# Three weight chunks' splits set behind the convolution's first-half taps and behind the first normalisation (two-layer decoder trunk, one core)

## The chip, the cores and the metric

The kernel runs on one core of a Trainium2 chip. The metric is device time of one execution in microseconds (us). The kernel before ran three times: 524.99 us median, 523.45 to 526.51.

## What is computed

Two residual layers over a stream of 512 tokens by 1024 channels. Layer 0 is attention; the change doesn't touch it. Layer 1, where the change lies, is cut here to what matters:

```python
def conformer_conv_layer(x, norm_g, w_in, conv_w, conv_b, ln_g, ln_b, w_out):
    h = rms_norm(x, norm_g)
    val, glu_gate, z = jnp.split(h @ w_in, 3, axis=-1)
    u = val * jax.nn.sigmoid(glu_gate)
    u = lax.conv_general_dilated(
        u, conv_w, window_strides=(1,), padding=((CONV_WIDTH - 1, 0),),
        dimension_numbers=('NWC', 'WIO', 'NWC'), feature_group_count=CONV_CH) + conv_b
    u = jax.nn.silu(layer_norm(u, ln_g, ln_b)) * jax.nn.silu(z)
    return x + u @ w_out
```

The convolution is depthwise and causal with 31 taps; the layer norm runs over all 1024 channels of a token, so no token can be normalised before the convolution of all eight channel tiles (128 channels each) is done for it.

## The kernel before

**Weights.** All weights are cut into 36 chunks of 1024 rows by 256 columns (1 MB). A chunk is loaded in fp32 into one of two buffers `wst` (`load_w`, line 152, issued by SyncE), and then split into a high and a low part (`split_w`, lines 155 to 180), since TensorE multiplies in a shorter float format and the kernel adds three products per matmul to get fp32 accuracy (`ch_mm`, `tok_mm`). Chunks 28 to 31 hold layer 1's columns for z; 33, 34, 32, 35 hold the output projection's four column groups 0, 1, 2, 3 (`OUTW`). For chunks 33, 34 and 35 the split is three steps: Pool issues a DMA that copies `wst` into the high part and rounds it (line 169: `whi` for 33 and 34, `wx` for 35); ScalarE writes minus the chunk into the low part (line 175: `wlo`, `wx`); Pool issues a second DMA that subtracts by adding `wst` onto it (line 179). Both DMAs go through Pool's one queue (q0 of the page). A `wst` buffer is free for the next load only when the ScalarE step and both DMAs are done. The function `ahead(n)` (lines 806 to 811) splits the chunks up to n-1 that are not split yet, and starts one more load after each: `ahead(34)` splits 33 and loads 34, `ahead(35)` splits 34 and loads 35, `ahead(36)` splits 35. With two buffers, 34 loads into the buffer of 32, and 35 into that of 33.

**Convolution.** Each channel tile's 31 taps are shared out: VectorE does some as multiply-adds into `s` (line 765), the rest are a ScalarE scaling into one of six buffers `tm` (line 774) and a Pool addition onto `pacc` (line 775; the first of these taps is written by ScalarE straight into `pacc`, line 771). VectorE adds both sums (line 782), TensorE transposes to token order (`conv_out`, line 795), VectorE takes statistics (line 797), ScalarE copies to `ctok` (line 798). The last two channel tiles, 6 and 7, are done in two halves of 256 tokens, so that the normalisation and projection of the first 256 tokens can start before the second half's convolution is done. The taps of their first half are written at lines 954 to 964, the z projections of chunks 28 to 30, with `ahead(34 + c)` after each, at 965 to 967.

**Order.** Up to line 1011 a scheduler orders each engine's queue. From line 1012 on the order of TensorE, VectorE, ScalarE and Pool is the order of the code: conv_out of tile 6 (first half), z of tile 6, conv_out of 7, the token statistics `norm_stats(0)` with the power of -0.5 on Pool (line 904, `lnr`), z of tile 7 in two pieces, `norm_cols` on VectorE (line 910), transposes back `ng_t` (line 921, `tp`), and then four rounds p = 0 to 3: ScalarE's SiLU (`ng_s`, line 927, `c`), VectorE's product with z (line 932), ScalarE's high part (`ng_u`, line 935, `u`), VectorE's low part (line 938), and TensorE's 24 output matmuls of the round for column groups 0 and 1 (line 360, into banks `st`, `o`, `mm`, `mm`). `na()` and `nd()` put the second half's taps between these, on ScalarE with Pool and on VectorE. Rounds 1 and 2 begin on TensorE with the transposes of the round after. Then come column groups 2 and 3, and the second half in the same way.

Of the kernel before, what the change touches and what calls it, by code (L numbers as in the profile page):

```python
# [13 lines left out]
AF = mybir.ActivationFunctionType  # L14
ALU = mybir.AluOpType
# [79 lines left out]
def tile_kernel(ctx: ExitStack, tc: tile.TileContext, x, xt, w, small0, small1, l1_norm, out):  # L95
# [7 lines left out]
    V, A, G, T, SY = nc.vector, nc.scalar, nc.gpsimd, nc.tensor, nc.sync  # L103
# [10 lines left out]
    def bank(tag, bufs):  # L114
        return ps.tile([P, 512], F32, tag=tag, name=tag, bufs=bufs)
# [4 lines left out]
    def stbank():  # L120

        return bank("st", 1)
# [8 lines left out]
    def sbank():  # L131
        return bank("s", 2)
# [94 lines left out]
    def fetch(i):  # L227
        if i < len(wsrc):
            raw[i] = load_w(*wsrc[i], 4 if i == 0 else 1)

    def split(i):
        if i < len(wsrc):
            wts[i] = split_w(raw.pop(i), rings[i], SPLIT_ENG(i, nc), APARTS if i in DMAS else 4 if i == 0 or 17 <= i < 24 else WPARTS, i in CAST)
# [34 lines left out]
    for i in range(2):  # L268
# [3 lines left out]
        for h in range(2):  # L272
            o, s = slice(8 * h, 8 * h + 8), slice(8 - 8 * h, 16 - 8 * h)
# [49 lines left out]
    for t in range(NT):  # L323
        hn = v0[:, (t % 2) * KC * P:(t % 2 + 1) * KC * P].rearrange("p (k t) -> p k t", k=KC)
        ts = slice(t * P, (t + 1) * P)
        for h in range(2):
            ks = slice(h * 4, h * 4 + 4)
            V.tensor_tensor(hn[:, ks], xts[t][:, ks], gcol[:, ks, None].to_broadcast([P, 4, P]),
                            op=ALU.mult)
            hp[2 * t + h] = hpart = A.activation(hhi[:, ks, ts], hn[:, ks], AF.Copy)  # L330
            V.tensor_tensor(hlo[:, ks, ts], hn[:, ks], hhi[:, ks, ts].bitcast(F32),
                            op=ALU.subtract)
        if t == 0:
            split(0)
    for t in range(NT):
        with tc.issue_after(hp[JO[t]].ins):
            A.activation(xs[t], xs[t], AF.Square, accum_out=ssx[:, t:t + 1])
        v = small.tile([P, 1], F32, tag="vv", name="vv")
# [127 lines left out]
    last = [None] * 4  # L466
# [280 lines left out]
    def conv_steps(ct, acc, pacc, n0, n):  # L747

        u = ups[ct % NU]
        nv = CONV - (POOLT[ct] if ct < KC - NLATE else POOLH[ct, n0 // HT])  # L750
        o = slice(n0, n0 + n)

        def tap(i):
            return u[:, OFF + i + n0:OFF + i + n0 + n], cw[:, ct, i:i + 1]

        first = []

        def vstep(i):
            v, w = tap(i)
            if i == 0:  # L760
                first.append(l1.tile([P, S], F32, tag="first", name="first", bufs=FB))
                V.tensor_scalar(first[0][:, :n], v, w, cbias[:, ct:ct + 1], op0=ALU.mult,
                                op1=ALU.add)
            else:
                V.scalar_tensor_tensor(acc[:, o], v, w, first[0][:, :n] if i == 1 else acc[:, o],  # L765
                                       op0=ALU.mult, op1=ALU.add)

        def astep(i):
            v, w = tap(i)
            if i == nv:  # L770
                A.activation(pacc[:, o], v, AF.Copy, scale=w)
                return
            tm = l1.tile([P, S], F32, tag="tm", name="tm", bufs=TMB)
            A.activation(tm[:, :n], v, AF.Copy, scale=w)  # L774
            G.tensor_tensor(pacc[:, o], pacc[:, o], tm[:, :n], op=ALU.add)  # L775

        return ([partial(vstep, i) for i in range(nv)],
                [partial(astep, i) for i in range(nv, CONV)])

    def conv_final(acc, pacc, n0, n):  # L780
        o = slice(n0, n0 + n)
        return lambda: V.tensor_tensor(pacc[:, o], acc[:, o], pacc[:, o], op=ALU.add)

    def conv(ct, acc, pacc, n0, n):
        v, a = conv_steps(ct, acc, pacc, n0, n)
        v[0]()
        a[0]()
        for f in v[1:] + a[1:]:
            f()
        last[3] = conv_final(acc, pacc, n0, n)()  # L790

    def conv_out(ct, pacc, t0=0, n=NT):
        pt = tpbank()
        for t in range(t0, t0 + n):
            last[1] = T.transpose(pt[:, t * P:(t + 1) * P], pacc[:, t * P:(t + 1) * P], identf)
        for t in range(t0, t0 + n):
            V.bn_stats(stats[:, t, ct, :], pt[:, t * P:(t + 1) * P])
        A.activation(ctok[:, t0:t0 + n, ct * P:(ct + 1) * P],
                     pt[:, t0 * P:(t0 + n) * P].rearrange("p (t c) -> p t c", t=n), AF.Copy)

    def new_pacc():
        return l1.tile([P, S], F32, tag="pacc", name="pacc", bufs=2)
# [3 lines left out]
    def ahead(n):  # L806
        while nsp[0] < n:
            split(nsp[0])
            nsp[0] += 1
            fetch(nf[0])  # L810
            nf[0] += 1
# [26 lines left out]
    def z_chunk(i, c):  # L838
        for j in range(2):
            z_unit(i, 2 * c + j)  # L840
# [39 lines left out]
    for c in range(1, 4):  # L880
# [4 lines left out]
        for j in range(2):  # L885
# [3 lines left out]
            acc, pacc = sbank(), new_pacc()  # L889
# [16 lines left out]
    def norm_cols(h, c):  # L906

        cs = slice(c * D // 2, (c + 1) * D // 2)
        for t in (2 * h, 2 * h + 1):
            V.tensor_scalar(ctok[:, t, cs], ctok[:, t, cs], mv[:, t, 0:1], rs[:, t:t + 1],  # L910
                            op0=ALU.subtract, op1=ALU.mult)
# [50 lines left out]
            f()  # L962
    for ct in late:
        conv_final(*ends[ct], 0, HT)()
    for c in range(3):
        z_chunk(28 + c, c)
        ahead(34 + c)

    (v6, a6), (v7, a7) = (conv_steps(ct, *ends[ct], HT, HT) for ct in late)
    vsteps = v6[:V6]  # L970
# [2 lines left out]
    n = max(len(v6), len(v7))  # L973
# [19 lines left out]
    def na():  # L993
        ca(next(aq))

    def nd():
        cv(next(dq))

    def z_mm(i, ct, po=None, ks=range(KC)):
        if po is None:  # L1000
            po = mmbank()
        ch_mm(po, nhi, nlo, wts[i], ct % 2, ks=ks)
        return po

    def z_act(ct, po):
        A.activation(zs[:, ct, :], po, AF.Silu)
# [5 lines left out]
    with tc.manual_schedule(engines=engs):  # L1012
        conv_out(6, ends[6][1], 0, 2)
        z6 = z_mm(31, 6, None, range(Z6))
        na()
        nd()
        conv_out(7, ends[7][1], 0, 2)
        z_mm(31, 6, z6, range(Z6, KC))
        na()
        z_act(6, z6)  # L1020
        norm_stats(0)
        z7 = z_mm(31, 7, None, range(ZK))
        na()
        nd()
        norm_cols(0, 0)
        ng_t(0, 0)
        ng_t(0, 1)
        z_mm(31, 7, z7, range(ZK, KC))
        norm_cols(0, 1)
        banks = [stbank(), bank("o", 1), bank("mm", 2), bank("mm", 2)]  # L1030
        units = [(c, t) for c in range(2) for t in range(2)]
        for p in range(4):
            k = 2 * p
            ng_s(0, k)
            ng_s(0, k + 1)
            na()
            nd()
            ng_m(0, k)
            ng_m(0, k + 1)
            ng_u(0, k)  # L1040
            ng_u(0, k + 1)
            if p == 0:
                z_act(7, z7)
            na()
            nd()
            ng_l(0, k)
            ng_l(0, k + 1)
            if p == C34:
                hi = main.tile([P, KC, WC], F32R, tag="big", name="hi", bufs=3)
                G.dma_start(hi.rearrange("p k n -> p (k n)"), w_ap(*wsrc[32], 0, KC))  # L1050
                wts[32] = hi, wts[32][1]
            if p in (1, 2):
                ng_t(0, p + 1)
            for (c, t), po in zip(units, banks):
                out1_mm(c, t, po, (2 * p, 2 * p + 1))
        for (c, t), po in zip(units, banks):
            out1_add(c, t, po)
        ca(99)
        cv(99)
        def unit(c, t, f=None):  # L1060
            po = mmbank()
            out1_mm(c, t, po)
            return lambda: out1_add(c, t, po)
        turn[0] = 0
        u = None
        for it in SEQ:
            w = None
            if it[0] == "c":
                conv_out(int(it[1]), ends[int(it[1])][1], 2, 2)
                if it == "c7":  # L1070
                    norm_stats(1)
            elif it == "n":
                norm_cols(1, 0)
                ng_t(1, 0)
                ng_t(1, 1)
                norm_cols(1, 1)
            else:
                w = unit(int(it[0]), int(it[1]))
            if u:
                u()  # L1080
            u = w
        for k in range(4):
            ng_s(1, k)
            ng_m(1, k)
            ng_u(1, k)
            ng_l(1, k)
            if k == 1 and u:
                u()
        units = [(c, 2 + t) for c in range(2) for t in range(2)]
        banks = [bank("mm", 2), bank("mm", 2), stbank(), bank("o", 1)]  # L1090
        for p in range(4):
            if p in (1, 2):
                ng_t(1, p + 1)
                for k in (2 * p + 2, 2 * p + 3):
                    ng_s(1, k)
                    ng_m(1, k)
                    ng_u(1, k)
                    ng_l(1, k)
            for (c, t), po in zip(units, banks):
                out1_mm(c, t, po, (2 * p, 2 * p + 1))  # L1100
        for (c, t), po in zip(units, banks):
            out1_add(c, t, po)
        turn[0] = 0
        for c in (2, 3):
            for t in (2, 3):
                unit(c, t)()
# [80 lines left out]
```

## Time and profile before

| | |
|---|---|
| median of three runs | 524.99 us (523.45 to 526.51) |
| the profiled execution | 525.7 us, of which the span of the trace is 523.9 us |
| granted TensorE clock, mean | 0.984 |
| busy: TensorE / weight loads / VectorE / ScalarE / Pool | 505.9 / 462.0 / 375.8 / 329.8 / 232.3 us |
| first half's taps, normalisation and rounds | about 424 to 482 us of the span |
| second half's | to 523.9 us |

The page divides the span into 40 slices of 13.1 us with the busy share of each engine in tenths. The waits view says who waited for whom, in us in total, number of times, and the longest. The chain of waits follows the last instruction back to what released it. The timeline lists instructions with start, length and, in brackets, the idle time before them with its releaser. The windows view gives busy time per engine, the granted clock (1.00 is full) and the share of the DMA engines for a stretch.

### The profile page before, as it was taken

What the parts mean: (1) busy time and instruction counts of PE and PEld (TensorE: products, weight loads), DVE (VectorE), ACT (ScalarE), POOL (GpSimd) and SP (SyncE); (2) the same over time, 40 slices, a digit from 0 to 9 for tenths busy, and PEclk for the clock granted to TensorE, in tenths of its full rate; (3) what the DMA queues carried; (4) which work ended last, traced back from release to release, by engine and by line L of the source; (5) the groups of instructions that cost most, each with busy time, mean ns of one, the idle gap of its engine ahead of it and who ended that gap; (6) DMA issues with size and microseconds to landing.
All of it is one profiled execution on the core that took longest, in us unless ns stands there. A gap on an engine that the chain in (4) does not pass through costs nothing.

```text
span 523.9 us, 9734 instructions
## 1 busy us (share of the span) xinstructions
PE 505.9 (97%) x3683; PEld 462.0 (88%) x3683; DVE 375.8 (72%) x788; ACT 329.8 (63%) x668; POOL 232.3 (44%) x255
## 2 busy tenths in 40 slices
PE   6999999999999999999999999999999999779997
PEld 3999998987889988788779999999999887559997
DVE  6856577856565587586696256999999997778741
ACT  3846687876555785576374735998686755478230
POOL 4166545010323143223202113879998875777200
PEclk8999999999999999999999999999999999879999
DMA  7742222202122233303219578488999799962111
GB/s 264 306 180 83 81 81 102 76 30 82 61 102 81 81 125 99 138 10 114 102 41 398 124 213 233 89 210 290 230 305 255 203 261 314 265 171 101 41 49 43
DMA packets 16566, 79.05 MB, mean 151 GB/s; under 512 B 1988, under 2 KB 4352, under 8 KB 8712
## 3 DMA queue, kind: packets, MB, share of 16 engines
q1 hardware_dynamic: 12776, 51.17, 26.8%
q0 software_dynamic: 3744, 27.26, 21.7%
q8 instruction: 29, 0.48, 0.4%
q14 instruction: 17, 0.14, 0.1%
HBM read 50.07 MB, written 2.14 MB: 100 GB/s over the span
## 4 chain that ended last, share of the span: by engine, by line
PE 72%; DMA 12%; DVE 5%; ACT 5%; POOL 3%; issue 2%; SPq 0%; POOLq 0%; ACTq 0%
PE mm L360 30%; DMA wst<-in_w_dram 7%; PE mm L369 6%; PE mm L370 6%; PE mm L371 6%; PE st L360 4%; PE o L602 3%; PE tp L525 3%; POOL pacc L775 2%; PE o L360 2%; PE s L509 2%; DMA lo<-wst 2%; PE s L511 2%; DMA wlo<-wst 2%; DMA wx<-wst 2%
## 5 line engine op out<-in xcount | busy, mean ns | idle before, releaser
L775 POOL TENSOR_TENSOR pacc<-pacc,tm 128x256 f32<-128x256 f32 (+1 forms) x125 | 120.2, 982 | 16.3 <-ACT tm L774 10.5
L765 DVE SCALAR_TENSOR_TENSOR s<-u,parts,s 128x256 f32<-128x256 f32 (+1 forms) x211 | 108.2, 571 | 0.5
L360 PE MATMUL mm<-whi,hhi 128*128 128x256 f32 (+1 forms) x352 | 100.2, 292 | 3.1 <-ACT hhi L330 2.9
L360 PE MATMUL mm<-whi,hlo 128*128 128x256 f32 (+1 forms) x352 | 99.4, 289 | 0.0
L360 PE MATMUL mm<-wlo,hhi 128*128 128x256 f32 (+1 forms) x352 | 99.0, 289 | 0.0
L774 ACT ACTIVATE tm<-u,parts 128x256 f32<-128x256 f32 (+1 forms) x125 | 66.2, 571 | 14.7 <-POOL pacc L775 14.2
L360 PEld LDWEIGHTS mm<-whi,hhi 128*128 128x128 f32 x352 | 66.9, 193 | 4.7 <-ACT hhi L330 3.4
L360 PEld LDWEIGHTS mm<-whi,hlo 128*128 128x128 f32 x352 | 66.7, 193 | 0.2
L360 PEld LDWEIGHTS mm<-wlo,hhi 128*128 128x128 f32 x352 | 66.6, 193 | 0.2
L173 ACT ACTIVATE whi<-wst 128x512 fp32r<-128x512 f32 (+2 forms) x77 | 49.3, 707 | 8.8 <-DMA wst<-in_w_dram 7.8
L522 ACT ACTIVATE p<-p,nm 128x128 f32<-128x128 f32 (+3 forms) x64 | 35.8, 559 | 26.9 <-DVE nm L521 26.3
L517 POOL TENSOR_TENSOR cb<-cb,mask 128x128 f32<-128x128 f32 x32 | 15.4, 485 | 77.4 <-DVE nm L521 48.8
L177 POOL TENSOR_TENSOR wlo<-wst,whi 128x512 fp32r<-128x512 f32 (+1 forms) x22 | 31.0, 1417 | 38.3 <-ACT whi L173 38.3
L177 DVE TENSOR_TENSOR wlo<-wst,whi 128x512 fp32r<-128x512 f32 (+1 forms) x50 | 40.4, 840 | 9.9 <-ACT whi L173 9.8
L369 PE MATMUL mm<-nhi,wx 128*128 128x256 f32 (+1 forms) x104 | 33.8, 325 | 0.0
L371 PE MATMUL mm<-nhi,wx 128*128 128x256 f32 (+1 forms) x104 | 32.9, 316 | 0.0
L370 PE MATMUL mm<-nlo,wx 128*128 128x256 f32 (+1 forms) x104 | 32.8, 316 | 0.0
L370 PE MATMUL mm<-nlo,whi 128*128 128x256 f32 (+1 forms) x104 | 31.9, 307 | 0.0
L369 PE MATMUL mm<-nhi,whi 128*128 128x256 f32 (+1 forms) x104 | 31.8, 307 | 0.0
L371 PE MATMUL mm<-nhi,wlo 128*128 128x256 f32 (+1 forms) x104 | 31.7, 306 | 0.0
L395 POOL TENSOR_TENSOR rq<-vq,mhalf 128x16 f32<-128x16 f32 x8 | 26.2, 3281 | 5.0 <-DVE vq L393 4.9
L525 PE MATMUL tp<-identf,p 128*128 128x128 f32 x160 | 28.1, 275 | 0.4 <-ACT pt L533 0.3
(292 smaller groups left out, 1434.8 us busy)
## 6 DMA issues: line engine op xcount, KB each, us to landing
wst<-in_w_dram SPq DMA_DIRECT2D x33, 1024.0 KB, 5.2
wx<-wst POOLq DMA_DIRECT2D x13, 1024.0 KB, 7.9
wlo<-wst POOLq DMA_DIRECT2D x8, 1024.0 KB, 8.9
whi<-wst POOLq DMA_DIRECT2D x3, 1024.0 KB, 5.9
wst<-in_w_dram SPq DMA_DIRECT2D x2, 1040.0 KB, 4.7
xs<-in_x_dram SPq DMA_DIRECT2D x4, 512.0 KB, 9.4
cb<-cdram SPq DMA_DIRECT2D x8, 256.0 KB, 3.7
x<-in_x_dram SPq DMA_DIRECT2D x4, 512.0 KB, 7.2
```

Of the source, the lines that this page charges most:

```text
L173: A.activation(hi[:, ks], st[:, ks], AF.Copy)
L177: (V if eng is G and parts == 4 and k % 4 and V0 else eng).tensor_tensor(lo[:, ks], st[:, ks], hi[:, ks].bitcast(F32), op=ALU.subtract)
L360: T.matmul(po, a[:, k, ts], b[:, k, :n], start=first and i == 0, stop=last and i == len(prods) - 1)
L369: T.matmul(po, whi[:, k, cs], a, start=k == 0, stop=False)
L370: T.matmul(po, whi[:, k, cs], b, start=False, stop=False)
L371: T.matmul(po, wlo[:, k, cs], a, start=False, stop=k == KC - 1)
L395: G.tensor_tensor(r, v, mhalf[:, :16].rearrange("p (t h) -> p t h", t=NT), op=ALU.pow)
L522: A.activation(p[:, :w], p[:, :w], AF.Exp, bias=nm, scale=-1.0, accum_out=sm[:, h, t:t + 1])
L525: T.transpose(tp[:, j * P:(j + 1) * P], p[:, j * P:(j + 1) * P], identf)
L765: V.scalar_tensor_tensor(acc[:, o], v, w, first[0][:, :n] if i == 1 else acc[:, o], op0=ALU.mult, op1=ALU.add)
L774: A.activation(tm[:, :n], v, AF.Copy, scale=w)
L775: G.tensor_tensor(pacc[:, o], pacc[:, o], tm[:, :n], op=ALU.add)
```

## The change

The splits of chunks 33 and 34 get a condition that they be issued only after the last first-half tap on ScalarE and on Pool (`taps`, the last ones of tile 7). The split of chunk 35 is taken out of the loop and put behind `norm_cols(0, 1)`, in the part whose order is the code's. `last[3]`, which held VectorE's final addition and was read nowhere, now holds the Pool tap.

```diff
-            A.activation(tm[:, :n], v, AF.Copy, scale=w)
-            G.tensor_tensor(pacc[:, o], pacc[:, o], tm[:, :n], op=ALU.add)
+            last[2] = A.activation(tm[:, :n], v, AF.Copy, scale=w)
+            last[3] = G.tensor_tensor(pacc[:, o], pacc[:, o], tm[:, :n], op=ALU.add)
...
-        last[3] = conv_final(acc, pacc, n0, n)()
+        conv_final(acc, pacc, n0, n)()
...
+    taps = last[2].ins, last[3].ins
     for c in range(3):
         z_chunk(28 + c, c)
-        ahead(34 + c)
+        if c < 2:
+            with tc.issue_after(taps[0]), tc.issue_after(taps[1]):
+                ahead(34 + c)
...
         z_mm(31, 7, z7, range(ZK, KC))
         norm_cols(0, 1)
+        ahead(36)
         banks = [stbank(), bank("o", 1), bank("mm", 2), bank("mm", 2)]
```

No instruction is added or taken away, and TensorE's, VectorE's and SyncE's queues keep their order. On Pool, in the stretch from the first half's taps to round 0, `pacc` rows are taps, `whi`, `wlo` and `wx` rows the DMAs of chunks 33, 34 and 35, `lnr` the power of the first half's norm:

```order
-L775 TENSOR_TENSOR pacc<-pacc,tm 128x256
+L775 TENSOR_TENSOR pacc<-pacc,tm 128x256 x15
 L169 DMA whi<-wst 128x2048
-L775 TENSOR_TENSOR pacc<-pacc,tm 128x256
 L179 DMA wlo<-wst 128x2048
 L169 DMA whi<-wst 128x2048
+L179 DMA wlo<-wst 128x2048
+L775 TENSOR_TENSOR pacc<-pacc,tm 128x256 x3
+L904 TENSOR_TENSOR lnr<-lnv,mhalf 128x2
+L775 TENSOR_TENSOR pacc<-pacc,tm 128x256 x7
+L169 DMA wx<-wst 128x2048
+L179 DMA wx<-wst 128x2048
```

The four DMAs of chunks 33 and 34, which stood among the taps, now stand together behind all of the first half's; the two of chunk 35, which stood ahead of `lnr`, stand behind it and behind seven of the second half's taps.

On ScalarE, at the end of that stretch, `wx` is the low part of chunk 35, `ctok` the copy of tile 7's first half, `zs` the SiLU of z of tile 6 and `c` the SiLU that opens round 0 (line 1006 has become 1010):

```order
-L175 ACTIVATE wx<-wst 128x2048
 L798 ACTIVATE ctok<-tp 128x2x128
-L1006 ACTIVATE zs<-mm 128x512
+L1010 ACTIVATE zs<-mm 128x512
 L774 ACTIVATE tm<-u_3240,parts 128x256 x7
+L175 ACTIVATE wx<-wst 128x2048
 L927 ACTIVATE c<-tp,parts 128x256 x2
```

Chunk 35's step stood ahead of the copy, and now stands directly ahead of round 0's SiLU. The two `wlo` steps of chunks 33 and 34 have likewise moved from among ScalarE's first-half taps to behind the last of them.

## Prediction

> **What bounds the kernel now.** First the page: TensorE is busy nearly all the time, so the holes in its row are the place to look.
>
> ```profile
> span 523.9 us, 9734 instructions
> PE 505.9 (97%) x3683; PEld 462.0 (88%) x3683; DVE 375.8 (72%) x788; ACT 329.8 (63%) x668; POOL 232.3 (44%) x255
> PE   6999999999999999999999999999999999779997
> ```
>
> The two 7s are 445 to 471 us, just where the change works. Next the waits, 420 to 500 us:
>
> ```profile
> DVE pacc L782 <- POOL pacc L775: 6.5, 3, 5.4
> ACT wx L175 <- DMA wst<-in_w_dram: 6.2, 1, 6.2
> DVE ctok L910 <- POOL lnr L904: 3.7, 2, 3.2
> PE tp L921 <- DVE ctok L910: 3.6, 2, 3.3
> PE tp L795 <- DVE pacc L782: 3.5, 1, 3.5
> ```
>
> TensorE has two holes. For 3.5 us it waits on VectorE's final sum, which waits on Pool's taps, which stand behind the DMAs of chunk 33 and 34 that wait for their loads. For 3.3 us it waits on the first norm, whose `lnr` stands on Pool behind chunk 35's DMA, which waits for ScalarE's step and that for its load. The chain that ended last says the same, and shows that one resource runs through it all: loads and copies of the weights.
>
> ```profile
> 424.56 10.89 DMA lo<-wst
> 435.52 6.04 DMA wst<-in_w_dram
> ...
> 449.05 9.78 DMA wst<-in_w_dram
> ...
> 469.04 1.50 PE st L360 x6
> ...
> 473.19 1.02 ACT c L927 x2
> ```
>
> After each hole TensorE's granted clock is halved (in these rows of the windows view it stands ahead of the DMA share and the GB/s):
>
> ```profile
> 449.10:452.50 3.40, 3.40 (x9) 2.62 (x9) 3.33 (x10) 2.76 (x8) 3.09 (x5) 0.51 1.15 255
> 462.70:469.50 6.80, 5.22 (x16) 3.85 (x16) 6.59 (x9) 4.01 (x11) 6.25 (x10) 0.51 0.83 177
> ```
>
> The first slow stretch lasts 3.4 us, the second 6.8.
>
> **What goes.** Pool, now:
>
> ```profile
> 425.17 9.52 POOL L775 TENSOR_TENSOR pacc<-pacc,tm 128x512 f32<-128x512 f32 x9
> 438.16 0.59 POOL L169 DMA_DIRECT2D whi<-wst  x1 [3.47 <-DMA wst<-in_w_dram]
> ...
> 446.49 9.12 POOL L775 TENSOR_TENSOR pacc<-pacc,tm 128x256 f32<-128x256 f32 x12 [0.21 <-ACT pacc L771]
> 459.39 0.59 POOL L169 DMA_DIRECT2D wx<-wst  x1 [3.78 <-DMA wst<-in_w_dram]
> ```
>
> With the DMAs behind the taps, Pool goes on at 434.7 (425.17 + 9.52). 14 first-half additions are left, five of tile 6 and nine of tile 7, at 0.76 us (9.12 / 12). Tile 6's final sum then waits only for VectorE, which before sat idle for its 5.4 us, so TensorE's 3.5 us and its half clock go. Tile 7's nine can't begin before ScalarE has written `pacc`, whose buffer TensorE frees at about 439.3:
>
> ```profile
> 438.74 0.60 PE L795 MATMUL tp<-identf,pacc 128*128 128x128 f32 x4
> ```
>
> and a SiLU stands ahead of that write on ScalarE; I allow 0.5 us for each and 0.1 for the passing on, so 440.45. They end at 440.45 + 9 x 0.76 = 447.3 (never waiting at all: 434.7 + 14 x 0.76 = 445.3). They ended at about 454.8 (446.49 + 11 x 0.76; the twelfth addition is of the second half). `lnr` no longer waits for chunk 35 either, so the norm comes 8 to 10 us earlier, and TensorE, which ended z of tile 7 at 468.5 (the `u` row below waits for it), is through with it at about 459. These savings, 3.5 + 3.3 us and most slow matmuls, count only if what follows is ready then.
>
> **What is late next.** Round 0 opens with ScalarE's `c`, and directly ahead of it now stands chunk 35's step, which needs the load. The load needs the buffer of chunk 33, whose two DMAs have moved behind 447.3. All later work on ScalarE, and so every round, stands behind that step. What the DMAs take (issue to landing, by windows around each issue; chunk 33's two, 34's two, 35's two):
>
> ```profile
> whi<-wst POOLq DMA_DIRECT2D x1, 1024.0 KB, 5.9
> wlo<-wst POOLq DMA_DIRECT2D x1, 1024.0 KB, 9.0
> whi<-wst POOLq DMA_DIRECT2D x1, 1024.0 KB, 9.2
> wlo<-wst POOLq DMA_DIRECT2D x1, 1024.0 KB, 14.0
> wx<-wst POOLq DMA_DIRECT2D x1, 1024.0 KB, 4.3
> wx<-wst POOLq DMA_DIRECT2D x1, 1024.0 KB, 8.2
> ```
>
> With these go the issue times 438.16, 439.91, 442.13, 443.85, 459.39 and 461.12:
>
> ```profile
> 439.91 0.87 POOL L179 DMA_DIRECT2D wlo<-wst  x1 [0.38 <-ACT wlo L175]
> 442.13 0.55 POOL L169 DMA_DIRECT2D whi<-wst  x1 [1.36 <-DMA wst<-in_w_dram]
> ...
> 443.85 0.87 POOL L179 DMA_DIRECT2D wlo<-wst  x1 [0.40 <-ACT wlo L175]
> ...
> 461.12 0.87 POOL L179 DMA_DIRECT2D wx<-wst  x1 [0.36 <-ACT ctok L798]
> ```
>
> Landings: 444.06, 448.9, 451.3, 457.85, 463.7, 469.3. They land in the order of issue, and the wait of `wst` ends at 448.9: chunk 35's load starts at 449.05. The first copy takes 4.3 us alone and 5.9 beside a load; I take 4.4, since chunk 34's load is long in by then. An adding DMA lands 4.85, 6.5 or 5.6 us behind the copy before it; I take 5.2, the mean of the two without a load beside them. The load takes 6.0 us (435.52) to 9.8 (449.05); I take 9.8, because this very load had chunk 34's two DMAs queued beside it then, and has again.
>
> The sum: 447.35 (first DMA issued) + 4.4 + 5.2 = 456.95, + 9.8 = 466.75 for the load, where it was 458.83. That is 7.9 us later. From there ScalarE:
>
> ```profile
> 458.91 1.91 ACT L175 ACTIVATE wx<-wst 128x2048 fp32r<-128x2048 f32 x1 [6.17 <-DMA wst<-in_w_dram]
> 460.73 0.36 ACT L798 ACTIVATE ctok<-tp 128x256 f32<-128x256 f32 x1
> ...
> 465.58 1.02 ACT L927 ACTIVATE c<-tp,parts 128x256 f32<-128x256 f32 x2 [1.22 <-PE tp L921]
> ...
> 468.57 0.76 ACT L935 ACTIVATE u<-c 128x256 fp32r<-128x256 f32 x2 [1.57 <-PE mm L370]
> ...
> 474.51 0.71 ACT L935 ACTIVATE u<-c 128x256 fp32r<-128x256 f32 x2
> ```
>
> The step starts 0.08 us after the load and holds ScalarE 1.82 us: `c` at 468.65, 3.1 us later than now. From `c` to `u` is 1.32 us where TensorE isn't waited for (473.19 to 474.51): 469.97. TensorE's first output matmul follows 0.47 us later (468.57 to 469.04): 470.4, so +1.4 us.
>
> The round itself: TensorE has by then been idle for some 11 us, three times the holes that halved its clock. The round's 24 matmuls and what they wait for took 3.46 us, from 469.04 to the next transposes, and only the first few were slow:
>
> ```profile
> 472.50 0.60 PE L921 MATMUL tp<-identf,ctok 128*128 128x128 f32 x4
> 471.24 1.41 PE mm L360 x12
> ```
>
> At full clock one takes 0.118 us (1.41 / 12), at the granted 0.51 0.23. If the slow stretch ends 3.4 us from the restart, 15 are slow and 9 quick, 4.5 us; if it lasts 6.8 us, all are slow, 5.5. I take 5.1, a little nearer to the second, whose stretch began like this one with an idle TensorE under a slow clock: +1.6 us. The transposes at its end come 3.0 us later, and they release `c` of round 2 and everything after it in the chain quoted. Nothing behind them has slack in which 3.0 us vanish: the second half's taps on ScalarE and Pool are queued between the same rounds.
>
> **Covers that hold.** Chunk 34's low part lands 457.85 - 448.9 = 8.95 us behind chunk 33's, at 465.9, before column group 1 is read at about 473. Chunk 35's low part would land at 466.85 + 4.3 + 5.6 = 476.8; its readers, the last column group, and those of column group 2's high part, whose load queues behind it, come after 482:
>
> ```profile
> L360 PE MATMUL mm<-hi,u x32: 279/282/363, 483.3 to 489.2; 128*128 128x256 f32 x32
> hi<-in_w_dram POOLq DMA_DIRECT2D x1, 1024.0 KB, 5.2
> ```
>
> 476.8 + 5.2 = 482.0 against 483.3 + 3.0. If this cover failed, it would cost its overrun there. The moved `wlo` steps cost nothing: ScalarE, which runs up to six buffers ahead of Pool, is done with the first half's taps 3 to 4 us before it, and the two steps fit in there at 1.8 us each.
>
> **The sum.** The profiled execution took 525.7 us, 523.9 of it span; it becomes 526.9 of span. The median before, 524.99, lies 0.7 below that execution, so I forecast 524.99 + 3.0 = 528.0 us. The bounds of the terms: landing at 447.35 + 4.3 + 4.85 + 6.04 = 462.5 with everything fast, which is 4.2 earlier (523.8), and 447.35 + 5.9 + 6.5 + 9.8 = 469.6 with everything slow, 2.9 later (530.9).
>
> **Rivals.**
>
> *Faster: the copies run at the pace of the quickest.* Chunk 34's copy landed 2.4 us after the DMA before it (451.3 - 448.9). If the adding ones also did once nothing else loads, chunk 33 is through at 447.35 + 4.3 + 2.4 = 454.05, the load takes 6.04, `c` comes at 460.2 + 1.82 = 462.0, TensorE restarts at 463.8 and, with 5.1 us for the round, reaches the transposes at 468.9 instead of 472.5: 3.6 us won, 521.4 us. It decides at a landing of 463.75, 3.0 us ahead of the sum's; earlier than that the change gains. The quick copy speaks for it; against it, none of three adding DMAs took under 4.85. The Trainium skill's "DMA: Bandwidth & Descriptors", section "Anatomy of one DMA — SWDGE (gpsimd) path", fits a Pool DMA as about 2.0 us plus its bytes over 436 GB/s, an estimated 4.4 us for 1 MB and 2.4 for each queued behind it, and has no term for adding. The trace agrees for the two copies (4.3 and 2.4) and not for the additions. Chance 0.14.
>
> *No change: the load is quicker than it was.* Copies as in the sum, the load at 7.57 us as an earlier one:
>
> ```profile
> 396.23 7.57 DMA wst<-in_w_dram
> ```
>
> It lands 2.2 us earlier, and the time is 525.8; at 6.04 it is 524.2. For it: loads elsewhere are that quick. Against: they weren't beside two queued Pool DMAs. Chance 0.29, with small shortfalls of other terms.
>
> *Much slower: the four DMAs run abreast.* If Pool's four shared the engines instead of following each other, chunk 33 would be through only with chunk 34, at about 465.9, and the load, now alone, would land at 472.0: 5.3 us more, 533.3. The landings in order of issue speak against it. Chance 0.05.
>
> That the change does nothing is excluded: the rows moved past one another.
>
> **How the numbers follow.** The forecast's case has 0.52; its own range is 526.2 to 530.9. About 0.5% of the time (2.6 us) is what a measurement of this kernel can tell from no change, so the line lies at 527.6, inside that case, with three parts of it in four above, where its longer tail is. Slower by over 0.5%: 0.39 of the case's 0.52 and the worst rival's 0.05, 0.44. Within 0.5%: the second rival's 0.29 and the case's other 0.13, less 0.02 for the quickest loads, 0.40. Faster: the first rival's 0.14 and these 0.02, 0.16. The range of 8 in 10 leaves out the fast rival's gain and the worst one's loss: from 522.6, about a us under the bound with everything fast, for the spread of the runs, to 530.9.
>
> **What would show it.** Right: Pool's first-half taps in one piece to 447, its four DMAs right behind; no TensorE wait ahead of tile 6's transposes; `lnr` near 453; ScalarE's `wx` step waiting about 10 us for `wst`, landing near 466.8; TensorE idle some 11 us to 470, then at half clock; `c` of round 2 near 476. Wrong: the landing before 464, a wait of TensorE for chunk 34 or column group 2, or `c` of round 0 released by TensorE's transposes.

## The result and the profile after

In what follows *before* and *after* are also the names of the two kernels.

| | before | after |
|---|---|---|
| median of four runs each | 524.45 us (523.45 to 526.51) | 530.94 us (530.67 to 531.61) |
| ratio | | 1.0112, 95% interval 1.0078 to 1.0146 |
| the profiled execution, its span | 525.7, 523.9 us | 530.67, 528.9 us |
| granted TensorE clock, mean | 0.984 | 0.981 |

Slower by 1.1%, about 5.9 us by the ratio (6.5 between the two medians of the table). The forecast was 528.0 us, its range 522.6 to 530.9: sign and mechanism were right, the size (3.0 us) was about half of what came, and the median lies 0.04 us above the range's top.

The page of after has one hole in TensorE's row where there were two slices with a 7, and it is deeper:

```profile
span 528.9 us, 9735 instructions
PE 504.0 (95%) x3683; PEld 460.9 (87%) x3683; DVE 374.9 (71%) x788; ACT 329.7 (62%) x668; POOL 233.7 (44%) x255
PE   6999999999999999999999999999999999539997
```

The slices with 5 and 3 are 450 to 476 us (the 35th and 36th of 40, 13.2 us each). Their cause, from the waits of after between 420 and 505 us (us in total, times, longest):

```profile
DVE c L932 <- ACT c L927: 15.2, 2, 12.1
...
PE st L360 <- ACT u L935: 13.4, 1, 13.4
ACT wx L175 <- DMA wst<-in_w_dram: 13.1, 1, 13.1
POOL wx L169 <- DMA wst<-in_w_dram: 9.6, 1, 9.6
```

The waits for Pool's taps and for `lnr` are gone, as planned. In their place ScalarE stands 13.1 us in front of chunk 35's step for the load of `wst`; TensorE waits 13.4 us for ScalarE's `u`, and VectorE 12.1 us for ScalarE's `c`. Three engines wait for one transfer. Pool's timeline shows where it comes from:

```profile
439.21 7.44 POOL L775 TENSOR_TENSOR pacc<-pacc,tm 128x256 f32<-128x256 f32 x9 [2.76 <-ACT pacc L771]
446.62 0.60 POOL L169 DMA_DIRECT2D whi<-wst  x1
447.21 0.89 POOL L179 DMA_DIRECT2D wlo<-wst  x1
447.75 0.91 POOL L169 DMA_DIRECT2D whi<-wst  x1
448.29 1.25 POOL L179 DMA_DIRECT2D wlo<-wst  x1
```

The four DMAs leave within two us. While the taps ran, there was nothing for the DMA engines: the windows view of after (length, the five engines' busy time, the clock, the DMA share, GB/s) has

```profile
441.00:446.60 5.60, 5.60 (x27) 4.56 (x26) 4.85 (x14) 5.35 (x7) 5.13 (x7) 1.00 0.00 0
```

a DMA share of 0.00 at 0 GB/s; the same 5.6 us had a share of 1.10 before. TensorE is busy in all of it, which is what the change won, and the transfers paid for it. The chain of after, from there to round 2:

```profile
447.21 8.88 DMA wlo<-wst
...
456.22 11.45 DMA wst<-in_w_dram
...
467.75 1.91 ACT wx L175
469.66 0.91 ACT c L927 x2
...
470.86 0.42 ACT u L935
...
478.15 1.02 ACT c L927 x2
```

Chunk 33's adding DMA, then the load into the buffer that it frees, then the split of chunk 35, then round 0. `c` of round 2 comes at 478.15, where it was 473.19: 4.96 us later, and the span is 5.0 us longer. So the whole loss of this trace lies ahead of that row, and nothing came or went behind it.

The restart, on TensorE:

```profile
471.32 0.58 PE L360 MATMUL st<-whi,u 128*128 128x256 f32 x1 [13.39 <-ACT u L935]
477.03 1.02 PE L921 MATMUL tp<-identf,ctok 128*128 128x128 f32 x4
471.30:477.03 5.73, 5.65 (x24) 5.36 (x25) 4.24 (x10) 3.47 (x9) 3.49 (x5) 0.50 1.16 227
```

All 24 matmuls of round 0 ran at a granted clock of 0.50 and took 5.7 us, against 3.46 before.

### The profile page after: what moved, and what is told of

Same layout as the page of the kernel before. It is cut to its first block, busy times and chain, and to the rows that moved or that the text cites. A ratio compares the mean times of both kernels' runs of the same rounds, so it can differ in the third digit from the quotient of the medians.

```text
span 528.9 us, 9735 instructions
## 1 busy us (share of the span) xinstructions
PE 504.0 (95%) x3683; PEld 460.9 (87%) x3683; DVE 374.9 (71%) x788; ACT 329.7 (62%) x668; POOL 233.7 (44%) x255
## 4 chain that ended last, share of the span: by engine, by line
PE 78%; DMA 7%; DVE 5%; ACT 4%; POOL 4%; issue 2%; SPq 0%; POOLq 0%; ACTq 0%; DVEq 0%
PE mm L360 30%; PE mm L369 7%; PE mm L370 7%; PE mm L371 7%; DMA wst<-in_w_dram 4%; PE st L360 4%; POOL pacc L775 3%; PE tp L525 3%; PE o L602 3%; PE o L360 2%; PE st L369 2%; PE st L370 2%; PE st L371 2%; PE s L509 2%; PE s L511 2%
## 5 line engine op out<-in xcount | busy, mean ns | idle before, releaser
L369 PE MATMUL mm<-nhi,wx 128*128 128x256 f32 (+1 forms) x104 | 32.6, 313 | 0.0
L371 PE MATMUL mm<-nhi,wx 128*128 128x256 f32 (+1 forms) x104 | 31.8, 305 | 0.0
```

The source lines that it names most:

```text
L369: T.matmul(po, whi[:, k, cs], a, start=k == 0, stop=False)
L371: T.matmul(po, wlo[:, k, cs], a, start=False, stop=k == KC - 1)
```

## The experiments

The theory: the loss is chunk 35's load, which starts late because chunk 33's DMAs stand behind the taps and which round 0 awaits because `c` stands behind the `wx` step on ScalarE; the half clock after the idle time adds to it. The rivals: the four DMAs cost as much wherever chunk 35 is split; the load is slow for a reason of its own; or the loss lies in chunk 35's own move. The experiments undo one half of the change at a time, move chunk 35 further, take the half clock away, and take traffic from beside the load. All medians, with the ratio to the kernel before; A to D and E to H were each run on one chip beside runs of before (median 525.44 us of 15 runs beside A to D, 525.57 of 25 beside E to H, 524.45 of 4 beside after):

| kernel | splits of 33, 34 | split of 35 | median, us | ratio | `c` of round 2, us | span, us |
|---|---|---|---|---|---|---|
| before | among the taps | ahead of `lnr` | 525.57 (25 runs) | 1 | 473.19 | 523.9 |
| after | behind the taps | behind the norm | 530.94 | 1.0112 | 478.15 | 528.9 |
| A | among the taps | behind the norm | 520.65 | 0.9912 [0.9883, 0.9941] | 467.57 | 518.6 |
| B | behind the taps | left to the scheduler: round 2 | 525.77 | 1.0006 [0.9991, 1.0022] | 472.01 | 524.4 |
| C | behind the taps | behind round 3 | 530.66 | 1.0106 [1.0072, 1.0140] | 470.33 | 527.3 |
| D | as after, TensorE kept busy | behind the norm | 528.73 | 1.0065 [1.0044, 1.0085] | 475.31 | 526.0 |
| E | behind the taps | behind round 1 | 523.93 | 0.9972 [0.9955, 0.9988] | 470.73 | 521.9 |
| F | among the taps | behind round 1 | 522.03 | 0.9935 [0.9908, 0.9961] | 468.81 | 519.5 |
| G | only 34 behind the taps | behind the norm | 520.76 | 0.9909 [0.9876, 0.9942] | 467.94 | 520.1 |
| H | as after, less one DMA | behind the norm | 526.22 | 1.0011 [0.9992, 1.0030] | 473.03 | 523.7 |

From `c` of round 2 to the end of the span it is 50.7 us before and after, and 50.7 to 52.4 in all the others but C, which has 57.0.

**A, chunk 35's move alone.**

```diff
-            with tc.issue_after(taps[0]), tc.issue_after(taps[1]):
-                ahead(34 + c)
+            ahead(34 + c)
```

> Only chunk 35's split is moved behind the first norm; 33 and 34 keep their old places among the taps. Theory (the load is late because chunk 33's DMAs are late): the load of 35 starts near 449 and lands near 459 as before the change, ScalarE's step is over at about 462, no longer late for round 0; the hole of 3.3 us ahead of the norm and its slow clock go, the hole of 3.5 us at tile 6 stays: about 5 us faster than before, 519.5 us. Rival (the step's place directly ahead of round 0 costs by itself, whenever the load comes): round 0 late, at least 3 us slower than before, 527 us or more.

Measured: 520.65 us, 0.9% faster than before. ScalarE's rows of A:

```profile
458.87 1.90 ACT L175 ACTIVATE wx<-wst 128x2048 fp32r<-128x2048 f32 x1
460.68 1.01 ACT L927 ACTIVATE c<-tp,parts 128x256 f32<-128x256 f32 x2
```

The `wx` step has no wait in brackets: the load, started at 446.87 and 10.9 us long, landed at 457.8, 1.1 us before ScalarE came to the step. So the half of the change that moves chunk 35 behind the norm is a gain, and `c` of round 0 can come at 460.68. One point of the expectation was wrong: the hole of 3.5 us at tile 6 didn't stay as it was. TensorE waits 1.6 us there and 1.7 at tile 7, and its granted clock is 1.00 from 440 to 480 us, where before it was halved twice.

**B, chunks 33 and 34 alone.**

```diff
+        else:
+            ahead(36)
...
-        ahead(36)
         banks = [stbank(), bank("o", 1), bank("mm", 2), bank("mm", 2)]
```

> Only 33 and 34 are moved behind the taps; 35's split is written in the loop again, without a condition, and the scheduler sets it on ScalarE in the middle of round 2. Theory: the load is as late as in the changed kernel (about 468), but rounds 0 and 1 don't stand behind it; TensorE now waits in round 0 for chunk 34's low part (about 467), and ScalarE's step holds round 2 for 1.8 us: 6 us faster than the changed kernel, about 524.5 us, near the time before. Rival (the four DMAs in a row are the cost, through chunk 34): as slow as the changed kernel, 530 us.

Measured: 525.77 us, no difference from before. Its waits name a second price of the late DMAs, one that after hides behind the first:

```profile
ACT c L927 <- PE tp L921: 13.2, 5, 7.6
```

ScalarE waits up to 7.6 us for TensorE's transposes, and TensorE's row shows what held these:

```profile
468.35 0.58 PE L360 MATMUL mm<-wlo,u 128*128 128x256 f32 x1 [4.83 <-DMA wlo<-wst]
```

Round 0 reaches column group 1 and waits 4.8 us for the low part of chunk 34, the last of the four DMAs. In after TensorE restarts only at 471.32, and that part landed at 466.8.

**C, chunk 35 behind round 3.**

```diff
-        ahead(36)
...
+            if p == 3:
+                ahead(36)
```

> The changed kernel with 35's split set behind round 3's steps instead of ahead of round 0. Theory: the load is as late as in the changed kernel and nobody waits for it; TensorE waits in round 0 for chunk 34's low part at about 467: 8 us faster than the changed kernel, 523 us. Rival (DMA crowding): 530 us. Rival (the place alone costs, by the 1.8 us of the step): 529 us.

Measured: 530.66 us, as slow as after; the theory missed. Up to round 2 it went as expected: `c` of round 2 at 470.33, 7.8 us ahead of after. All but 1.6 us of that was lost behind it (528.9 to 527.3). Chunk 35's adding DMA was issued at 480.23 and landed 11.54 us later, at 491.77; in after it was issued at 469.96 and took 8.7. So of the 13.1 us by which it lands later, 10.3 are its later issue and 2.8 a longer transfer, beside the output's first writes. TensorE's last column group waited for it, with the second half's transposes queued behind. The chain of C, and two of its waits:

```profile
480.23 11.54 DMA wx<-wst
...
491.81 4.38 PE st L360 x23
496.20 0.87 PE tp L921 x8
```

```profile
PE mm L360 <- DMA wlo<-wst: 4.6, 1, 4.6
...
PE st L360 <- DMA wx<-wst: 3.9, 1, 3.9
```

The cover for chunk 35's parts, which holds in after, was overrun. The first of the two waits is B's; behind it `c` of round 2 was still early. The second was not made good, and behind it TensorE's granted clock was 0.50 from 491.8 to 494.9.

**D, TensorE kept busy.** 56 matmuls whose result nobody uses stand ahead of round 0.

```diff
+        for i in range(56):
+            T.matmul(banks[0], wts[33][0][:, i % KC, :P], nhi[:, i % KC, :], start=True, stop=True)
```

> The changed kernel with 56 extra matmuls of 512 columns (about 13 us at full clock) into a bank that round 0 overwrites, between z of tile 7 and round 0, so that TensorE doesn't idle; they add nothing to the output. Theory (of the changed kernel's loss, about 2.8 us is the half clock in round 0): round 0 takes 3 us instead of 5.7, 2.5 to 3 us faster than the changed kernel, about 528 us. Rival (the load alone sets the end, the clock is covered by ScalarE's steps): as the changed kernel, 531 us.

Measured: 528.73 us, near the theory's 528. ScalarE waits the same 13.1 us, and the round's matmuls run at full clock:

```profile
471.00:474.50 3.50, 3.10 (x24) 2.89 (x24) 3.33 (x8) 3.50 (x10) 2.10 (x4) 1.00 1.09 253
```

Its first output matmul starts at 471.06 and its transposes at 474.61, 3.55 us against 5.71 in after. So the half clock costs after 2.2 us, in the round as between the medians (2.8 between the profiled executions, where D also restarts 0.3 us earlier). What is left goes with the late load, as A and G show.

**E, chunk 35 one round later** (`if p == 1: ahead(36)` in C's place).

> After, with chunk 35's split one round later, behind round 1 on ScalarE and Pool. Theory (the loss is that c of round 0 stands behind the wx step of chunk 35 on ScalarE, whose load is late): rounds 0 and 1 run from about 461 us and need only chunks 0 to 31 and 33; the wx step runs at the load's landing, about 467.7 to 469.6, shortly ahead of c of round 2, which comes near 470 instead of 478.15; chunk 35's two DMAs land near 477 to 480, ahead of its matmuls in the last column group. The end comes about 8 us earlier than after, 523 us. Rival (the first half's later start is paid in any place, as it was with the split at round 3): the last column group waits 3 to 5 us for chunk 35's parts and the time stays at 528 to 531 us.

Measured: 523.93 us, 7 us below after and a little faster than before. The median agrees with the theory's 523, but one point of the expectation was wrong: rounds 0 and 1 don't need chunk 33 alone, each round multiplies with column groups 0 and 1, and so with chunk 34 too:

```profile
467.00 0.58 PE L360 MATMUL mm<-wlo,u 128*128 128x256 f32 x1 [5.15 <-DMA wlo<-wst]
```

This is B's wait again, 5.15 us, and TensorE's clock is at 0.50 behind it (467.0 to 472.1). `c` of round 0 comes at 456.28, earlier than A's 460.68, and `c` of round 2 at 470.73, later than A's 467.57: between the two lies this wait. E is 3.2 us behind A there and 3.3 at the end. The wait for chunk 35 was 13.1 us on ScalarE in after; here it is 5.9 us, and passes while TensorE waits for chunk 34. The move to round 1 avoids the first price, not the second.

**F, chunk 35 behind round 1, chunks 33 and 34 in their old places.**

> Chunks 33 and 34 split where the kernel before had them, chunk 35 alone moved, behind round 1. Theory: the load has landed long before (as with chunk 35 alone behind the norm, 520.65 us), so one round later costs ScalarE nothing and chunk 35's parts still land ahead of their use: 520 to 521.5 us. Rival (the last column group is at its limit already, each us later shows): 523 to 525 us.

Measured: 522.03 us (520.23 to 525.45), half a us over the theory's band and under the rival's. Its interval overlaps A's; that the later place costs something is not shown.

**G, chunk 33 in its old place, only chunk 34 behind the taps.**

```diff
-        if c < 2:
+        if c == 0:
+            ahead(34)
+        elif c == 1:
             with tc.issue_after(taps[0]), tc.issue_after(taps[1]):
-                ahead(34 + c)
+                ahead(35)
```

> Chunk 33 split where the kernel before had it, 34 behind the last taps, 35 behind the norm: two SBUF to SBUF DMAs behind the taps instead of four. Theory (the load of chunk 35 waits for the buffer that chunk 33's adding DMA frees last): that buffer is free before the taps end, the load runs ahead of 448 us or thereabouts, the wx step waits for nothing, c of round 0 comes near 460.5: 519 to 521 us, as with chunk 35 alone moved. Rival (the DMAs behind the taps and the load crowd each other whatever their number, and the wx step waits to 464 or later): 526 to 529 us.

Measured: 520.76 us, A's time. Chunk 33's adding DMA is issued at 440.41 and takes 8.5 us, and the load that follows it, ahead of chunk 34's DMAs (issued from 453.31), takes 4.7; ScalarE doesn't wait for it:

```profile
wst<-in_w_dram SPq DMA_DIRECT2D x1, 1024.0 KB, 4.7
459.16 1.90 ACT L175 ACTIVATE wx<-wst 128x2048 fp32r<-128x2048 f32 x1
460.97 1.00 ACT L927 ACTIVATE c<-tp,parts 128x256 f32<-128x256 f32 x2
```

So the whole loss of after against A, 10.3 us between the medians, hangs on the place of chunk 33's split. Chunk 34's place behind the taps, with chunk 33's DMAs out of its way, costs nothing that this can tell. It gains nothing either.

**H, less traffic beside the load.** Chunk 34's adding DMA is left out (`add` is false for this chunk alone). Its low part then holds minus the chunk where the small remainder belongs; the matmuls are as many as in after.

```diff
-        if eng is None:
+        if eng is None and add:
```

> After without chunk 34's second DMA, the adding one, so that column group 1 lacks chunk 34's low part in its weights. It takes 1 MB of traffic from beside chunk 35's load. Theory (the load took 11.45 us because that DMA ran beside it): the load takes 7 to 8 us, lands near 464, the wx step ends near 466, 3.5 us ahead of after: 527 us. Rival (the load is slow for a reason of its own, or was slow beside the copies alone): it takes 11 us again and the time is 530.5 us.

Measured: 526.22 us, 4.7 below after. The chain of H:

```profile
448.07 8.84 DMA wlo<-wst
...
457.05 6.72 DMA wst<-in_w_dram
...
463.85 1.91 ACT wx L175
```

The load takes 6.72 us instead of 11.45. So 4.7 of after's 11.45 us are the adding DMA beside it; the theory had the load at 7 to 8 us. Chunk 33's pair took the same time (8.84 against 8.88). The restart came sooner too, after 8.9 us idle, and of round 0's matmuls the last third ran at full clock (from 471.4): `c` of round 2 at 473.03, 5.1 us ahead of after.

Not tried: a third `wst` buffer, with which chunk 35's load wouldn't have to wait for chunk 33's split.

## Why the prediction was right in its direction and short in its size

**What goes.** Right. The taps ran without a DMA between them to 446.6 (forecast 447.3), with one wait of 2.76 us for ScalarE's `pacc`, tile 6's transposes waited for nothing, the norm came near 452 (`lnr`; forecast 453), and TensorE had no work left at 457.9 (forecast 459). It then stood idle for 13.4 us, and ScalarE for 13.1 at the `wx` step, where the forecast had some 11 and about 10: TensorE was ready 1.1 us sooner and ScalarE about 2, and the load came 0.9 later.

```profile
443.94 0.38 PE L795 MATMUL tp<-identf,pacc 128*128 128x128 f32 x2
452.03 0.72 POOL L904 TENSOR_TENSOR lnr<-lnv,mhalf 128x2 f32<-128x2 f32 x1
```

What the earlier norm is worth where `c` doesn't wait for the load, C and E show: `c` of round 0 at 455.97 and 456.28, where it was 465.58 before. Neither could keep it, since the same late DMAs hold round 0's column group 1.

**What is late next.** Right: ScalarE's `wx` step, and with it every round. The terms, forecast and measured:

| term | forecast | after |
|---|---|---|
| first DMA issued | 447.35 | 446.62 |
| chunk 33's copy | 4.4 | 4.5 |
| its adding DMA, behind the copy | 5.2 | 5.0 |
| chunk 35's load | 9.8 | 11.45 |
| load lands | 466.75 | 467.67 |
| `c` of round 0 | 468.65 | 469.56 |
| first output matmul | 470.4 | 471.32 |
| round 0's 24 matmuls | 5.1 | 5.7 |
| transposes of round 2 | 475.5 | 477.03 |

Two terms were mis-sized. **The load**, "9.8, because this very load had chunk 34's two DMAs queued beside it then, and has again": it had, but the pair itself was slower. Chunk 34's two DMAs landed 10.7 us behind chunk 33's (456.09 to 466.8), where they took 8.95 before, and in both traces the load ends about a us behind them (458.83 against 457.85 before, 467.67 against 466.8 after). The issue to landing of chunk 34's two in after:

```profile
whi<-wst POOLq DMA_DIRECT2D x1, 1024.0 KB, 11.9
wlo<-wst POOLq DMA_DIRECT2D x1, 1024.0 KB, 18.5
```

H shows what the load would have been without the adding one: 6.72 us. The forecast took 9.8 us for its bound with everything slow too, from one row of one trace. That row was a short one: in A and F, where the pair stands in its old place, the load beside it took 10.9 and 11.0 us, so 1.1 to 1.2 of the 1.65 us appear without the move. D, with the DMAs as in after, has 11.5; in B, C and E the load took 12.4 to 12.5, but there Pool's load for column group 2 was queued behind the pair as well (in E issued at 459.9, landed 10.4 us later). Why the pair took less in before's trace stays open.

**The round**: bounded by 4.5 and 5.5 and taken at 5.1, it came to 5.7. The clock stayed at half for 6.5 us from the restart (471.3 to about 477.8), near the longer of the two stretches, and the transposes behind it ran slow as well (1.1 us from their start to `c`, where it was 0.7). The Trainium skill's "TensorE: Matmul & The Clock Gate", section "Part 1: The HAM clock gate", has a free-running window of about 3.4 us, a full busy one of which brings the clock back; an estimate from this is that a restart is slow for 3.4 to 6.8 us, as it falls. The traces agree in the main: from the restart to the full clock it took 6.5 us in after, 4.0 in H (467.4 to 471.4) and 5.8 behind the second hole of before (463.87 to 469.7), but only 3.1 in C's last column group (491.8 to 494.9).

**The sum.** The profiled executions differ by 5.0 us where the forecast had 3.0: of the 2.0 more, 0.9 is the landing, 0.6 the matmuls, 0.4 the transposes. The other 1.0 of the 2.9 us by which the median missed (530.94 - 528.0) lies in the step from the profiled time to the median: the price was worked out in an execution of 525.7 us and then set on a median 0.7 lower, as if the execution's surplus stayed, and after's median came 0.3 above its own profiled execution. A likely reason why it didn't stay is that before's profiled execution had been late already ahead of the change; tile 5's statistics on VectorE in before, and then in after:

```profile
439.73 0.89 DVE L797 BATCH_NORM_STATS2 stats<-tp 128x6 f32<-128x128 f32 x4
```

```profile
438.57 0.89 DVE L797 BATCH_NORM_STATS2 stats<-tp 128x6 f32<-128x128 f32 x4 [0.59 <-PE tp L795]
```

That is 1.2 us (0.8 at TensorE's transposes for them, 438.74 against 437.94) which the two traces' difference doesn't show, and with it the change would cost 5.8 to 6.1 us, near the 5.9 of the ratio. One trace of each is no proof of it.

**Nothing behind has slack.** Right: 50.7 us from `c` of round 2 to the end, before and after.

**Covers that hold.** Right for after, and narrow. Chunk 34's low part landed at 466.8 (forecast 465.9), but B and E, which start round 0 earlier, wait 4.8 and 5.15 us for it. Chunk 35's parts were in time at the place the forecast was made for, and not at C's.

**The rivals.** *Faster* would have needed a landing before 463.75, and chunk 33's adding DMA at 2.4 us; it took 5.0. The page "DMA: Bandwidth & Descriptors" of the Trainium skill, in "Anatomy of one DMA — SWDGE (gpsimd) path", has a fit from which these 2.4 us can be estimated, 4.4 for a first DMA of 1 MB and 2.4 for each queued behind it. The trace agrees for the first copy, 4.5 us, and not for what followed: 5.0, 3.6 and 7.1 us. *No change* needed a load of 6 to 7.6 us; in H it takes 6.72, lands at 463.77, and the time is 526.22 us with a ratio whose interval holds 1. That rival was worked out rightly, and fell to what was argued against it, the traffic beside the load. *Much slower* needed Pool's DMAs abreast; they landed in their order.

## What to carry to other kernels

A split that frees a buffer is the first link of the next load. Before such a step is moved to take its wait out of an engine's queue, follow the buffer to the work that stands behind the load, and ask what the DMA engines do in between: here they had nothing to do for 5.6 us, and then four transfers queued at once and the load beside the last two. And where a change has two halves, price each alone: moving chunk 35's split behind the norm won 0.9% by itself, moving chunk 33's behind the taps turned that into a loss, and leaving chunk 33 in its place (A, G) keeps the gain.

## What the runs showed of the hardware that was not expected

- A load on SyncE's queue and Pool's queued DMAs slow each other: the 1 MB load took 4.7 us with nothing beside it (G), 6.72 beside a copy (H), and 9.8 to 11.5 beside a copy and an adding DMA (9.8 in before, 10.9 in A, 11.0 in F, 11.45 in after, 11.5 in D), where it landed about 1 us behind the adding DMA.
- An adding DMA of 1 MB within on-chip memory landed 5.0 us behind its copy with no load beside it and 7.1 with the load (both in after), and 7.0 beside the output's writes (C).
- After 13.4 us without a matmul the granted clock was still at 0.50 for the next 6.5 us; 56 matmuls whose result nobody uses, in the idle time, held it at 1.00 and were worth 2.2 us (D).
